# Summing modulation vectors over partitions: VectorE transpositions and four small matmuls in place of one-hot matmuls

## The chip, the cores and the metric

The kernel runs on one core of one Trainium2 chip. The time is device microseconds of one execution on that core; the time before is the median of three runs. A profile of one further execution is read below. TensorE is the matmul engine, VectorE and ScalarE the two elementwise engines, SyncE (SP) the queue that issues nearly all loads.

## The reference

Two layers of a diffusion transformer work on 256 latent tokens `x` and 256 context tokens `ctx`, both 1024 wide and in float32. Each layer is a SwiGLU feed-forward, a mixer (attention, pooling, Fourier) and a second feed-forward. Nine modulation vectors of 1024 values, each for the latent stream (from `c`) and for the context stream (from `c_ctx`), shift, scale and gate them:

```python
mx = jnp.split(jax.nn.silu(c) @ ada_w[layer] + ada_b[layer], N_MOD, axis=-1)
mc = jnp.split((jax.nn.silu(c_ctx) @ ada_w[layer] + ada_b[layer])[None, :], N_MOD, axis=-1)
x = x + 0.5 * mx[2][:, None] * swiglu(modulate(rms_norm(x), mx[0], mx[1]), ffn1_w_gu[layer], ffn1_w_down[layer])
...                                   # the same for ctx with mc, then the mixer and the second feed-forward
return rms_norm(x) * final_gain
```

`ada_w` is (2, 1024, 9216). The change concerns how `silu(c) @ ada_w` is summed, nothing else.

## The kernel before

Activations lie transposed in `xT`: 128 partitions by 8 chunks of 1024 features by 512 columns (256 latent, 256 context tokens). Every large matmul is done three times, on a high and a low half of each operand in float32r (`mm3`, L404 to L406). Weights come through a feeder: SP loads blocks `raw` of 1 MB, ScalarE rounds a half block to `a` (L193), VectorE subtracts to get the low half (L171).

A feed-forward (`ffn`) runs a gate/up loop over 22 blocks of 128 hidden features, two at a time. For each, VectorE multiplies the gate by the up product out of PSUM (L701), ScalarE rounds it, VectorE subtracts the low half (L706). After blocks 5, 9, 13 and 17 a batch of the down projection runs (`down`), whose results VectorE scales by a gate from `modT` and adds to `xT` (L738). Behind the loop come `down(16, 18)` and `down(18, 22)`.

The modulation vectors of a feed-forward's groups are computed beside the loop, on VectorE: `ada_stream` loads blocks of 128 x 1024 of `ada_w` into two buffers `ada` (SP, L584). A block k is the k-th 128 rows of one vector's matrix; it multiplies by a column of `c32` and adds into an accumulator of 128 x 1024, one for each stream that needs the vector (L603 for the first block, L605 for the other seven). A unit is 16 such products for two accumulators. What is left is a sum over the 128 partitions: `ada_post`, once for each unit, does four matmuls with one-hot columns `hot` (L629), which put the sums into one row of each quarter of a PSUM bank; after the group's last unit ScalarE copies the bank, four matmuls transpose it (L641) and VectorE adds the bias into `modT` (L647). There are 14 units with 28 accumulators in six groups: three groups of one, three and three units (14 accumulators) beside the first feed-forward of layer 0, one of three beside its second, and two of three and one beside the first of layer 1.

What sets the order is a planner in Python, `Sched`: `S.pe(ns)` advances its clock by what a piece of TensorE work is meant to take, and tasks written as generators are resumed when their `yield`ed delay is over on that clock. Each engine's queue is then as the program was recorded. `ada_stream` yields `ada_pace` between products (2200 ns in layer 0's first feed-forward), and `need_ada` runs whatever is still missing at once, all delays left out. Such calls stand before `down` (L722) and behind the gate/up loop, for all groups of this feed-forward:

```python
for group in ada_groups[l, w]:
    for unit in group:
        for l_, m_, _ in unit:
            need_ada(l_, m_)
preload(AF.Sqrt)
feed.limit = 8
down(16, 18, [streams], False)
```

Of the kernel before, what the change touches and what calls it, by code (L numbers as in the profile page):

```python
# [10 lines left out]
F32 = mybir.dt.float32  # L11
F32R = mybir.dt.float32r
AF = mybir.ActivationFunctionType
ALU = mybir.AluOpType
AX = mybir.AxisListType

P = 128
D = 1024
KD = D // P
# [210 lines left out]
def tile_hybrid_dit(  # L230
# [7 lines left out]
    nc = tc.nc  # L238
    cst = ctx.enter_context(tc.tile_pool(name="cst", bufs=1))
    wp = ctx.enter_context(tc.tile_pool(name="wp", bufs=1))  # L240
    sb = ctx.enter_context(tc.tile_pool(name="sb", bufs=1))
    psp = ctx.enter_context(tc.tile_pool(name="psp", bufs=8, space=bass.MemoryType.PSUM))
    ctx.enter_context(tc.manual_schedule())
    S = Sched()
    uid = [0]

    def nid(s):
        uid[0] += 1
        return f"{s}{uid[0]}"

    def psum():
        return psp.tile([P, 512], F32, name=nid("ps"), tag="ps")

    def t2(dt=F32, w=512):
        return sb.tile([P, w], dt, name=nid("t2_"), tag="t2", bufs=T2_BUFS)

    def t1(dt=F32, w=256):
        return sb.tile([P, w], dt, name=nid("t1_"), tag="t1", bufs=6)

    def a4(dt=F32, w=1024):  # L260
        return sb.tile([P, w], dt, name=nid("a4_"), tag="a4", bufs=TILE_BUFS)
# [7 lines left out]
    mm = nc.tensor.matmul  # L269
# [3 lines left out]
    ident = small[:, 0:128]  # L273
# [3 lines left out]
    chC = small[:, 512:640]  # L277
    chS = small[:, 640:768]
    sel = small[:, 768:770]
    hot = cst.tile([P, 3, 32], F32, name="hot", tag="hot")  # L280
    epsb = cst.tile([P, 1], F32, name="epsb", tag="epsb")
    dummy = cst.tile([P, 2], F32, name="dummy", tag="dummy")
    c32 = cst.tile([P, KD, 32], F32, name="c32", tag="c32")
    modT = [cst.tile([P, 72, 2], F32, name=f"modT{l}", tag=f"modT{l}") for l in range(2)]
    vecT = [cst.tile([P, 82], F32, name=f"vecT{l}", tag=f"vecT{l}") for l in range(2)]
# [249 lines left out]
    ada_run = {}  # L535

    def mod_fix(l, m, c0, c1, ss=(0, 1)):
        v = modT[l][:, c0:c1, ss[0]:ss[-1] + 1]
        if m in (1, 4, 7):
            nc.vector.tensor_scalar_add(v, v, 1.0)  # L540
        if m in (2, 8):
            nc.vector.tensor_scalar_mul(v, v, 0.5)
# [29 lines left out]
    def ada_stream(groups, pace):  # L572
        blocks = [
            (g, n, e, k) for g in range(len(groups)) for n in range(len(groups[g]))
            for e in range(len(groups[g][n])) for k in range(KD)
        ]
        loaded = {}

        def load(i):
            if i < len(blocks):  # L580
                g, n, e, k = blocks[i]
                l, m, _ = groups[g][n][e]
                raw = sb.tile([P, 1024], F32, name=nid("ada"), tag="ada", bufs=ADA_BUFS)
                nc.sync.dma_start(out=raw, in_=ada_w[l, k * P:(k + 1) * P, m * 1024:(m + 1) * 1024])  # L584
                loaded[i] = (raw, S.t)

        for i in range(ADA_BUFS):
            load(i)
        for i, (g, n, e, k) in enumerate(blocks):
            l, m, ss = groups[g][n][e]  # L590
            if k == 0:
                if e == 0:
                    accs = []
                    if n == 0:
                        sums, bank = [], []
                accs.extend((a4(), l, m, s) for s in ss)
            raw, at = loaded.pop(i)
            while S.t < at + ADA_LAG and not force[0]:
                yield pace
            for acc, _, _, s in accs[-len(ss):]:  # L600
                sc = c32[:, k, s:s + 1]
                if k == 0:
                    nc.vector.tensor_scalar_mul(acc, raw, sc)  # L603
                else:
                    nc.vector.scalar_tensor_tensor(  # L605
                        out=acc, in0=raw, scalar=sc, in1=acc, op0=ALU.mult, op1=ALU.add,
                    )
                yield pace if i >= 8 else min(pace, 1400)
            load(i + ADA_BUFS)
            if k == KD - 1 and e == len(groups[g][n]) - 1:  # L610
                more = n < len(groups[g]) - 1
                task = S.add(ada_post(groups[g], n, accs, bank, list(sums)), 4000)
                accs = None
                sums.append(task)
                if not more:
                    for unit in groups[g]:
                        for l_, m_, _ in unit:
                            ada_run[l_, m_] = task

    def ada_post(group, n, accs, bank, before):  # L620

        for task in before:
            S.finish(task)
        last = n == len(group) - 1
        if not bank:
            bank.append(psum())
        ps = bank[0]
        for j in range(4):
            mm(ps[32 * j:32 * j + 32, :], hot[:, n, :], accs[j % 2][0][:, (j // 2) * 512:(j // 2 + 1) * 512],  # L629
               start=(n == 0), stop=last)  # L630
        S.pe(925)
        bank.append([(None,) + slot[1:] for slot in accs])
        del accs
        if not last:
            return
        sbt = t2()
        nc.scalar.copy(sbt, ps)
        yield 2000
        tp = psum()
        for i in range(4):  # L640
            nc.tensor.transpose(tp[:, i * P:(i + 1) * P], sbt[:, i * P:(i + 1) * P], ident)  # L641
        S.pe(4 * 117)
        t4 = tp.rearrange("p (i u s r) -> p i u s r", i=4, u=2, s=2)
        for r, slots in enumerate(bank[1:]):
            for j, (_, l, m, s) in enumerate(slots):
                c0 = m * 8
                nc.vector.tensor_tensor(  # L647
                    out=modT[l][:, c0:c0 + 8, s].rearrange("p (u i) -> p i u", u=2),
                    in0=t4[:, :, :, j, r],
                    in1=vecT[l][:, c0:c0 + 8].rearrange("p (u i) -> p i u", u=2),  # L650
                    op=ALU.add,
                )
        for unit in group:
            for l, m, ss in unit:
                mod_fix(l, m, m * 8, m * 8 + 8, ss)
                ada_ok.add((l, m))
# [19 lines left out]
    def ffn(l, w, streams, h_tasks, tail, early=None):  # L676
# [7 lines left out]
        def start_ada():  # L684
            if ada_groups[l, w]:
                ada_run["task"] = S.add(ada_stream(ada_groups[l, w], ada_pace[l, w]), 500)
# [557 lines left out]
    nc.vector.memset(epsb, EPS)  # L1244
    nc.vector.memset(dummy, 0.5)
    nc.vector.memset(c32, 0.0)
    nc.vector.memset(hot, 0.0)
    for n in range(3):
        nc.vector.memset(hot[:, n, n:n + 1], 1.0)
    zero = t1()  # L1250
    nc.vector.memset(zero, 0.0)
    ada_first(0)
# [2 lines left out]
    ada_first(1)  # L1255
    pc = psum()
    nc.tensor.transpose(pc[:, :16], crow[:16, :], ident[:16, :16])
    nc.scalar.activation(
        out=c32[:, :, 0:2], in_=pc[:, 0:16].rearrange("p (s k) -> p k s", s=2), func=AF.Silu
    )  # L1260
# [91 lines left out]
    for l in range(2):  # L1352
        last = l == 1
# [257 lines left out]
```

## Time and profile before

| | |
|---|---|
| median of 3 runs | 1603.69 us (1601.97 to 1603.72) |
| profiled execution | 1601.59 us, its span 1599.5 us |
| TensorE busy | 1579.3 us, 99% of the span |
| VectorE busy | 1078.4 us, 67% |
| ScalarE busy | 601.5 us, 38% |
| chain of work that ended last | TensorE 96%, VectorE 2% |

Busy time of matmuls is modelled, and neighbours overlap: a 128x512 matmul is listed with some 390 ns, and the next starts 227 ns later. So for TensorE the starts, or the pieces of the chain, tell what an instruction displaces. A matmul on plain float32 operands stands in two records. An idle time in brackets names the instruction that ended it.

### The profile page before, as it was taken

To read this page: it belongs to the slowest core of one execution; us is meant where nothing else is said; L and a number is where in the kernel's file an instruction comes from. 1 tells how busy PE (TensorE), PEld (TensorE's weight loads), DVE (VectorE), ACT (ScalarE), POOL (GpSimd) and SP (SyncE) were. 2 spreads that over 40 slices of the span, in tenths; PEclk is the share of its full clock that TensorE was granted. 3 is DMA by queue.
4 is the path that set the end of the run, shared out by engine and by line. 5 is a ranking of instruction groups with operands and counts; after the bars stand their busy time and mean duration, and the time that the engine had idled before them with its cause. 6 is when DMAs were issued, how large, how long until landed. Compare 5 with 4: busy or idle time off the path is not lost.

```text
span 1599.5 us, 20723 instructions
## 1 busy us (share of the span) xinstructions
PE 1579.3 (99%) x8359; PEld 1321.1 (83%) x8359; DVE 1078.4 (67%) x1672; ACT 601.5 (38%) x1003; POOL 0.8 (0%) x6
## 2 busy tenths in 40 slices
PE   7999999999999999999999999999999999999998
PEld 5888888888886898888888898888888898788886
DVE  4787878786857566766734576766656488776665
ACT  4422132123548452222222343232132356755554
POOL 0000000000000000000000000000000000000000
PEclk9999999999999999999999999999999999999999
DMA  9755465553012424534333315455555233346560
GB/s 333 258 182 203 141 236 174 194 187 117 33 42 66 132 106 159 180 132 159 112 112 106 107 58 185 165 194 201 184 203 178 83 110 95 116 150 229 188 208 30
DMA packets 149343, 241.68 MB, mean 151 GB/s; under 512 B 6484, under 2 KB 115712, under 8 KB 148992
## 3 DMA queue, kind: packets, MB, share of 16 engines
q1 hardware_dynamic: 147008, 238.71, 44.8%
q10 hardware_dynamic: 2240, 1.65, 0.3%
q8 instruction: 66, 1.08, 0.3%
q14 instruction: 29, 0.24, 0.0%
HBM read 239.30 MB, written 1.05 MB: 150 GB/s over the span
## 4 chain that ended last, share of the span: by engine, by line
PE 96%; DVE 2%; SPq 1%; DMA 1%; ACT 0%; issue 0%; ACTq 0%
PE ps L404 24%; PE ps L405 24%; PE ps L406 24%; PE ps L1376 5%; PE ps L1380 3%; PE ps L944 2%; PE ps L946 2%; PE ps L945 2%; PE ps L1165 1%; PE ps L1142 1%; PE ps L1430 1%; PE ps L1432 1%; PE ps L1431 1%; PE ps L629 1%; DMA a<-in_ada_w_dram 1%; SPq L304 1%
## 5 line engine op out<-in xcount | busy, mean ns | idle before, releaser
L404 PE MATMUL ps<-ahi,a 128*128 128x512 f32 (+1 forms) x1312 | 479.6, 366 | 0.8 <-ACT a L193 0.6
L405 PE MATMUL ps<-alo,a 128*128 128x512 f32 (+1 forms) x1312 | 477.2, 364 | 1.4 <-DVE alo L510 1.3
L406 PE MATMUL ps<-ahi,a 128*128 128x512 f32 (+1 forms) x1312 | 476.8, 363 | 1.5 <-DVE a L171 1.5
L171 DVE TENSOR_TENSOR a<-raw,a 128x1024 fp32r<-128x1024 f32 x300 | 361.6, 1222 | 144.6 <-ACT a L193 144.6
L193 ACT CAST a<-raw 128x1024 fp32r<-128x1024 f32 x300 | 304.5, 1044 | 200.7 <-PE ps L405 77.0
L404 PEld LDWEIGHTS ps<-ahi,a 128*128 128x128 f32 x1312 | 247.5, 189 | 48.0 <-issue 8.3
L605 DVE SCALAR_TENSOR_TENSOR a<-ada,c,a 128x1024 f32<-128x1024 f32 x196 | 249.0, 1279 | 48.0 <-DMA ada<-in_ada_w_dram 48.0
L405 PEld LDWEIGHTS ps<-alo,a 128*128 128x128 f32 x1312 | 247.6, 189 | 40.8 <-DVE alo L510 2.6
L406 PEld LDWEIGHTS ps<-ahi,a 128*128 128x128 f32 x1312 | 247.5, 189 | 40.9 <-DVE a L171 1.9
L404 PE MATMUL ps<-a,a 128*128 128x512 f32 (+1 forms) x624 | 223.8, 359 | 0.0
L406 PE MATMUL ps<-a,a 128*128 128x512 f32 (+1 forms) x624 | 222.5, 356 | 0.0
L405 PE MATMUL ps<-a,a 128*128 128x512 f32 (+1 forms) x624 | 222.4, 356 | 0.0
L738 DVE SCALAR_TENSOR_TENSOR xT<-ps,modT,xT 128x256 f32<-128x256 f32 x288 | 126.5, 479 | 74.0 <-PE ps L406 73.9
L703 ACT CAST a<-t 128x512 fp32r<-128x512 f32 x66 | 41.0, 622 | 269.0 <-DVE t L701 269.0
L404 PEld LDWEIGHTS ps<-a,a 128*128 128x128 f32 x624 | 117.9, 189 | 21.7 <-issue 5.0
L406 PEld LDWEIGHTS ps<-a,a 128*128 128x128 f32 x624 | 117.9, 189 | 17.0
L405 PEld LDWEIGHTS ps<-a,a 128*128 128x128 f32 x624 | 117.9, 189 | 16.8
L696 ACT ACTIVATE t<-ps 128x512 f32<-128x512 f32 x66 | 39.3, 599 | 223.4 <-PE ps L406 219.9
L701 DVE TENSOR_TENSOR t<-ps,t 128x512 f32<-128x512 f32 x66 | 45.3, 690 | 70.8 <-PE ps L406 63.4
L1376 PE MATMUL ps<-ahi,a 128*128 128x512 f32 x352 | 90.5, 392 | 0.7 <-DVE ahi L510 0.7
L1376 PEld LDWEIGHTS ps<-ahi,a 128*128 128x128 f32 x352 | 63.6, 189 | 12.0 <-DVE ahi L510 0.9
L506 ACT ACTIVATE ahi<-t,modT 128x256 fp32r<-128x256 f32 x88 | 43.6, 508 | 55.3 <-DVE t L503 55.2
(175 smaller groups left out, 1376.1 us busy)
## 6 DMA issues: line engine op xcount, KB each, us to landing
raw<-in_ffn_w_gu_dram SPq DMA_DIRECT2D x88, 1024.0 KB, 5.2
ada<-in_ada_w_dram SPq DMA_DIRECT2D x128, 512.0 KB, 5.5
raw<-in_ffn_w_down_dram SPq DMA_DIRECT2D x44, 1024.0 KB, 4.9
raw<-in_w_in_dram SPq DMA_DIRECT2D x10, 1024.0 KB, 5.2
a<-in_ada_w_dram SPq DMA_DIRECT2D x16, 512.0 KB, 10.0
raw<-in_w_out_dram SPq DMA_DIRECT2D x16, 256.0 KB, 4.4
raw<-in_w_out_dram SPq DMA_DIRECT2D x8, 512.0 KB, 5.4
raw<-tab_pool SPq DMA_DIRECT2D x2, 1024.0 KB, 4.8
```

What stands on the lines that cost most here:

```text
L171: self.nc.vector.tensor_sub(vl, src, vh.bitcast(F32))
L193: self.nc.scalar.copy(vh, src)
L404: mm(ps, whi, mhi, start=start, stop=False)
L405: mm(ps, whi, mlo, start=False, stop=False)
L406: mm(ps, wlo, mhi, start=False, stop=stop)
L506: nc.scalar.activation(out=ahi[:, d, seg_cols(s)], in_=t, func=AF.Identity, bias=mod(l, m, d, s))
L605: nc.vector.scalar_tensor_tensor(out=acc, in0=raw, scalar=sc, in1=acc, op0=ALU.mult, op1=ALU.add,)
L701: nc.vector.tensor_mul(a[:, :n], u[:, :n], sg[:, :n])
L703: nc.scalar.copy(at[:, 0:n], a[:, :n])
L738: nc.vector.scalar_tensor_tensor(out=xs, in0=ps[:, q * 256:(q + 1) * 256], scalar=mod(l, m0 + 2, d, s), in1=xs, op0=ALU.mult, op1=ALU.add,)
L1376: mm(ps, wt[0][:, k, :], ahi[:, k, :], start=(k == 0), stop=(k == KD - 1))
L1380: mm(ps[:, 0:256], wt[1][:, k, :], ahi[:, k, 0:256], start=False, stop=False)
```

## The change

The one-hot matmuls, the copy on ScalarE and the four transposing matmuls go. As soon as a unit's eighth block is added, each accumulator is taken in two halves of 128 x 512: VectorE transposes its 32 x 32 blocks into a `t2` buffer, then sums each row of 32 into 16 columns of `red`. Between these four instructions the stream yields 700 ns each. Only after a group's last unit does `ada_post` run: four matmuls with `fold` (128 x 32, four identity blocks under each other) add the four partition quarters, and VectorE adds the bias.

```diff
-                task = S.add(ada_post(groups[g], n, accs, bank, list(sums)), 4000)
...
+            if k == KD - 1:
+                for acc, l_, m_, s in accs[-len(ss):]:
+                    for h in range(2):
+                        tb = t2()
+                        nc.vector.transpose(tb, acc[:, h * 512:(h + 1) * 512])
+                        yield 700
+                        nc.vector.tensor_reduce(
+                            out=red[:, len(slots), h * 16:(h + 1) * 16], in_=tb.rearrange("p (b i) -> p b i", i=32),
+                            axis=AX.X, op=ALU.add,
+                        )
+                        yield 700
+                    slots.append((l_, m_, s))
+                if e == len(groups[g][n]) - 1:
+                    accs = None
+                    if n == len(groups[g]) - 1:
+                        task = S.add(ada_post(groups[g], red, list(slots)), 4000)
...
-    def ada_post(group, n, accs, bank, before):
...
-        for j in range(4):
-            mm(ps[32 * j:32 * j + 32, :], hot[:, n, :], accs[j % 2][0][:, (j // 2) * 512:(j // 2 + 1) * 512],
-               start=(n == 0), stop=last)
-        S.pe(925)
...
-        nc.scalar.copy(sbt, ps)
-        yield 2000
...
-            nc.tensor.transpose(tp[:, i * P:(i + 1) * P], sbt[:, i * P:(i + 1) * P], ident)
-        S.pe(4 * 117)
...
+    def ada_post(group, red, slots):
+
+        ps = psum()
+        n = len(slots)
+        for b in range(4):
+            mm(ps[32 * b:32 * b + 32, 0:n * 8].rearrange("p (n i) -> p n i", n=n), fold, red[:, 0:n, b:32:4],
+               start=True, stop=True)
+        S.pe(400)
+        yield 600
```

Where the planner's clock advances otherwise, the order moves. On VectorE, at the end of layer 0's first gate/up loop, before (`ps_2840` is the loop's last product, `a_376` an accumulator of the last unit, `ps_2880` the transposed sums):

```order
L605 SCALAR_TENSOR_TENSOR a_375_2521<-ada_2760,c_73,a_375_2521 128x1024
L605 SCALAR_TENSOR_TENSOR a_376_2522<-ada_2760,c_73,a_376_2522 128x1024
L171 TENSOR_TENSOR a_419_2809<-raw_2633,a_418_2808 128x1024
L701 TENSOR_TENSOR t_420_2836<-ps_2804,t_412_2769 128x512
L706 TENSOR_TENSOR a_421_2838<-t_420_2836,a_421_2838 128x512
L171 TENSOR_TENSOR a_424_2845<-raw_2671,a_423_2844 128x1024
L701 TENSOR_TENSOR t_426_2876<-ps_2840,t_416_2802 128x512
L647 TENSOR_TENSOR modT_74<-ps_2880,vecT_76 128x4x2 x6
```

The last two products of the last unit stand ahead of two more L701; behind the loop's last L701 comes the bias addition at once.

On VectorE at the same place, now (`ps_2836` is the loop's last product; `a_385`, `a_386` are the accumulators of the unit before the last, `a_441`, `a_442` those of the last):

```order
L603 SCALAR_TENSOR_TENSOR a_386_2554<-ada_2789,c_73,a_386_2554 128x1024
L615 STREAM_TRANSPOSE t_435_2866<-a_385_2553 128x512
L693 TENSOR_TENSOR t_436_2871<-ps_2836,t_424_2795 128x512
L617 TENSOR_REDUCE red_2208<-t_435_2866 128x16
L615 STREAM_TRANSPOSE t_438_2876<-a_385_2553 128x512
L617 TENSOR_REDUCE red_2208<-t_438_2876 128x16
L615 STREAM_TRANSPOSE t_439_2879<-a_386_2554 128x512
L617 TENSOR_REDUCE red_2208<-t_439_2879 128x16
L615 STREAM_TRANSPOSE t_440_2882<-a_386_2554 128x512
L617 TENSOR_REDUCE red_2208<-t_440_2882 128x16
L601 TENSOR_SCALAR a_441_2885<-ada_2826,c_73 128x1024
L601 TENSOR_SCALAR a_442_2886<-ada_2826,c_73 128x1024
```

Behind these stand fourteen products (L603 now, L605 before) for blocks two to eight of the last unit, then four transpositions with their row sums, then the bias addition; L693 is what was L701.

On TensorE, now, at the end of the same loop:

```order
L406 MATMUL ps_2836<-ahi,a_405_2652 128x512
L636 MATMUL ps_2927<-red_2208,fold 32x48 x4
L404 MATMUL ps_2942<-a_362_2372,a_410_2690 128x512
L405 MATMUL ps_2942<-a_362_2372,a_410_2690 128x512
L406 MATMUL ps_2942<-a_362_2372,a_411_2691 128x512
```

The four matmuls that read `red` stand between the loop's last matmul and the first of `down(16, 18)`; before, the one-hot matmuls stood 9 matmuls ahead of the loop's end and the four transpositions here.

## Rows read from the trace of the kernel before

**Rows 1.** The page: span, engines (share, instructions), granted clock in 40 slices.

```profile
span 1599.5 us, 20723 instructions
...
PE 1579.3 (99%) x8359; PEld 1321.1 (83%) x8359; DVE 1078.4 (67%) x1672; ACT 601.5 (38%) x1003; POOL 0.8 (0%) x6
...
PEclk9999999999999999999999999999999999999999
```

**Rows 2.** Groups by line: count, busy us, mean ns, idle before.

```profile
L605 DVE SCALAR_TENSOR_TENSOR a<-ada,c,a 128x1024 f32<-128x1024 f32 x196 | 249.0, 1279 | 48.0 <-DMA ada<-in_ada_w_dram 48.0
...
L701 DVE TENSOR_TENSOR t<-ps,t 128x512 f32<-128x512 f32 x66 | 45.3, 690 | 70.8 <-PE ps L406 63.4 <-ACT t L696 7.3
...
L1118 DVE TENSOR_REDUCE st<-ps 128x1 f32<-128x512 f32 (+1 forms) x40 | 27.2, 687 | 8.9 <-PE ps L1115 8.7
...
L603 DVE TENSOR_SCALAR a<-ada,c 128x1024 f32<-128x1024 f32 x28 | 20.7, 748 | 4.9 <-DMA ada<-in_ada_w_dram 4.8
...
L629 PE MATMUL ps<-a,hot 128*32 128x512 f32 x112 | 14.9, 605 | 0.0
...
L641 PE MATMUL ps<-small,t 128*128 128x128 f32 x24 | 3.6, 271 | 0.0
```

**Rows 3.** Chain that ended last, in order: start us, us, engine and line.

```profile
31.77 0.80 PE ps L561 x8
...
370.41 1.00 PE ps L629 x8
371.41 0.43 PE ps L404
371.84 0.23 PE ps L405
...
373.68 0.44 PE ps L641 x4
```

**Rows 4.** VectorE in order of time, 362 to 375 us: start us, us, instruction.

```profile
362.07 2.48 DVE L605 SCALAR_TENSOR_TENSOR a<-ada,c,a 128x1024 f32<-128x1024 f32 x2 [3.10 <-DMA ada<-in_ada_w_dram]
...
373.72 0.69 DVE L701 TENSOR_TENSOR t<-ps,t 128x512 f32<-128x512 f32 x1 [3.06 <-PE ps L406]
374.33 0.53 DVE L647 TENSOR_TENSOR modT<-ps,vecT 128x8 f32<-128x8 f32 x6
```

**Rows 5.** TensorE in order of time, near 5, 22 and 104 us.

```profile
4.76 0.26 PE L1257 MATMUL ps<-small,t 16*128 16x16 f32 x1 [4.76 <-DMA small<-tab_small]
...
22.55 0.38 PE L406 MATMUL ps<-ahi,a 128*128 128x256 f32 x1 [0.76 <-DVE a L171]
22.77 0.28 PE L404 MATMUL ps<-ahi,a 128*128 128x256 f32 x1
...
104.54 0.39 PE L404 MATMUL ps<-a,a 128*128 128x512 f32 x1
```

**Rows 6.** Landings of the `ada` loads: all; 299 to 310; 330 to 370 us.

```profile
DMA to landing us min/median/max: 3.4/5.5/10.0
...
DMA to landing us min/median/max: 4.6/4.6/4.6
...
DMA to landing us min/median/max: 5.6/6.0/6.3
```

**Rows 7.** VectorE in order of time, 95 to 101 us.

```profile
95.95 1.22 DVE L171 TENSOR_TENSOR a<-raw,a 128x1024 fp32r<-128x1024 f32 x1
97.09 0.75 DVE L603 TENSOR_SCALAR a<-ada,c 128x1024 f32<-128x1024 f32 x1
97.75 0.69 DVE L701 TENSOR_TENSOR t<-ps,t 128x512 f32<-128x512 f32 x1
99.12 0.69 DVE L706 TENSOR_TENSOR a<-t,a 128x512 fp32r<-128x512 f32 x1 [0.68 <-ACT a L703]
100.07 1.23 DVE L171 TENSOR_TENSOR a<-raw,a 128x1024 fp32r<-128x1024 f32 x1 [0.26 <-ACT a L193]
```

**Rows 8.** Stretch: us, then PE, PEld, DVE, ACT, POOL busy us, clock, DMA, GB/s.

```profile
108.00:340.00 232.00, 232.00 (x1040) 187.48 (x1039) 183.81 (x220) 54.24 (x67) 0.00 (x0) 1.00 0.53 184
```

More of the change, by code (lines that the diff above doesn't have):

```diff
@@ L279, in tile_hybrid_dit @@
     sel = small[:, 768:770]
-    hot = cst.tile([P, 3, 32], F32, name="hot", tag="hot")
+    fold = cst.tile([P, 32], F32, name="fold", tag="fold")
     epsb = cst.tile([P, 1], F32, name="epsb", tag="epsb")
@@ L593, in ada_stream @@
                     accs = []
-                    if n == 0:
-                        sums, bank = [], []
                 accs.extend((a4(), l, m, s) for s in ss)
@@ L609, in ada_stream @@
             load(i + ADA_BUFS)
-            if k == KD - 1 and e == len(groups[g][n]) - 1:
-                more = n < len(groups[g]) - 1
-                task = S.add(ada_post(groups[g], n, accs, bank, list(sums)), 4000)
[L613 to L618, printed above, removed]
-    def ada_post(group, n, accs, bank, before):
[L622 to L627, printed above, removed]
-        for j in range(4):
-            mm(ps[32 * j:32 * j + 32, :], hot[:, n, :], accs[j % 2][0][:, (j // 2) * 512:(j // 2 + 1) * 512],
-               start=(n == 0), stop=last)
-        S.pe(925)
[L632 to L636, printed above, removed]
-        nc.scalar.copy(sbt, ps)
-        yield 2000
-        tp = psum()
-        for i in range(4):
-            nc.tensor.transpose(tp[:, i * P:(i + 1) * P], sbt[:, i * P:(i + 1) * P], ident)
-        S.pe(4 * 117)
[L643 to L652, printed above, removed]
@@ new lines, in ada_stream @@
+            if k == 0 and e == 0 and n == 0:
+                red = sb.tile([P, 6, 32], F32, name=nid("red"), tag="red", bufs=1)
+                slots = []
+            if k == KD - 1:
[14 more added lines that the diff above has]
+                        task = S.add(ada_post(groups[g], red, list(slots)), 4000)
+                        for unit in groups[g]:
+                            for l_, m_, _ in unit:
+                                ada_run[l_, m_] = task
@@ new lines, in ada_post @@
+    def ada_post(group, red, slots):
[6 more added lines that the diff above has]
+        yield 600
+        for j, (l, m, s) in enumerate(slots):
+            c0 = m * 8
+            nc.vector.tensor_tensor(
+                out=modT[l][:, c0:c0 + 8, s], in0=ps[:, j * 8:j * 8 + 8], in1=vecT[l][:, c0:c0 + 8], op=ALU.add,
+            )
@@ L1246, in tile_hybrid_dit @@
     nc.vector.memset(c32, 0.0)
-    nc.vector.memset(hot, 0.0)
-    for n in range(3):
-        nc.vector.memset(hot[:, n, n:n + 1], 1.0)
     zero = t1()
@@ L1257, in tile_hybrid_dit @@
     nc.tensor.transpose(pc[:, :16], crow[:16, :], ident[:16, :16])
+    nc.vector.tensor_reduce(
+        out=fold, in_=ident.rearrange("p (a j) -> p j a", a=4), axis=AX.X, op=ALU.add,
+    )
     nc.scalar.activation(
```

## The prediction

> **What bounds the kernel now.** I read the page first [rows 1]: TensorE is busy for 1579.3 of 1599.5 us, VectorE for 67%, and the granted clock is full in every slice. So a microsecond taken off TensorE's queue is a microsecond off the end, and one of VectorE costs nothing unless TensorE has to wait for its result. Then I read the groups by line [rows 2] for prices, the chain of waits around one modulation post for what it displaces [rows 3], and the end of the first feed-forward's gate/up loop on VectorE [rows 4], because there the order of the changed kernel differs most. The profiled execution took 1601.59 us, its span and 2.1 us around it; the median of the runs shown is 1603.69. I add the sum to the median.
>
> **Taken off TensorE.** A post is eight records of L629 and takes 1.00 us of the chain; the matmul behind it takes 0.43 where its neighbours take 0.23, so a post displaces 1.20 us [rows 3]. There are 112 records [rows 2], that is 14 posts: 14 x 1.20 = 16.8. The four transpositions of L641 displace 0.44 [rows 3]; there are 24 of them, in six groups: 2.6. Together 19.4 us leave a queue that is always full. The six copies on ScalarE (L637) go too; ScalarE is 38% busy, so they are worth nothing.
>
> **Put on TensorE.** Six times four small matmuls with `fold`, eight records each time. No row shows their shape. Eight records with two columns take 0.80 [rows 3]; four transpositions 0.44; a whole post 1.20. I take 0.7 (0.4 to 1.2), nearest to the first: 6 x 0.7 = 4.2 us.
>
> **Put on VectorE.** Each of 28 accumulators gets two 32x32 transpositions and two row sums of 128x512. For the row sum L1118 has the form: 687 ns [rows 2]. A transposition stands in no row; the bounds are half of L603 (0.37) and one L605 (1.28), and I take 0.69, the 128x512 add of L701, also one element read and one written per lane. A sum waits for its transposition just ahead, so a pair costs about 1.3; instructions that wait for nothing follow at 0.1 less than their length (L605 in twos: 2.48). The Trainium skill (VectorE: DVE Perf Modes, The three transpose paths) gives 311 ns for a 128x128 bf16 transposition; four of these would make 1.24 us, an estimate, and the sum would be 3.9 higher. No row here tests it.
>
> All 112 come to some 72 us of VectorE. Where nobody waits they are free. What matters is where they stand.
>
> **The place that decides: the end of the first gate/up loop.** The stream of layer 0 runs on the planner's clock. Each accumulator now yields four times 700 ns, 2.8 us, and this stream has 14: 39 us more. Before, its last block was done at 362.07 + 2.48 = 364.5 us and the loop's last product started at 373.72 [rows 4], a spare of 9.2. So it is now 30 us late, about one unit (eight blocks by two products by 2.2 us: 35). The order says the same: all eight blocks of the last unit stand behind the loop's last product, forced out by `need_ada` before `down(16, 18)`, and the four fold matmuls stand on TensorE between the loop's last matmul and that `down`. Before, nothing of the kind stood there: TensorE went on, and VectorE waited 3.06 us for it [rows 4].
>
> TensorE then waits for the whole run, as matmuls are not taken past a waiting one (the L406 that waited 0.76 for VectorE held the L404 behind it [rows 5]). The run can't start earlier, since VectorE's multiplication (L701) ahead of it waits for that last matmul. From the moment it ends: the multiplication 0.6; one sum and three pairs of the unit before, 0.6 + 3.9; two L603, 1.3. That is 6.4. Fourteen L605 at 1.2 are 16.8, the last four pairs 5.2: 28.4 us if no weights are waited for. But two buffers hold the blocks, and a load is issued only when VectorE has finished with the block two earlier. From issue to landing the rows have 3.4 at least, 5.5 in the middle, 4.6 for one that followed a larger load [rows 6]; in the run no other load is issued, so I take 4.0, with 0.2 for the two hand-overs. A pair of blocks then takes 2.4 + 4.2 = 6.6: the third block starts at 6.4 + 4.2 = 10.6, the fifth at 17.2, the seventh at 23.8, the eighth ends at 28.6, the pairs at 33.8. **TensorE waits 34 us** (no load waited for and the cheap transposition: 26; landings of 6.3, the longest near this place [rows 6]: 41; with the dear transposition 45).
>
> Behind the run on VectorE stand the correction of the last activation and the splits for `down(18, 22)`; `down(16, 18)` needs neither for its 48 matmuls, and its weights were split ahead. The next weight loads on SP are released by these splits and so move with TensorE: nothing more is lost.
>
> **The first fold.** It stands behind the matmul that ended the sixth gate/up block, before `down(0, 4)`. There VectorE has no slack: it went from L171 through L603 to the product at 97.75, waited 0.68 for ScalarE, and took the next split at 100.07 [rows 7]. With eight instructions more between 96.0 and TensorE's arrival (104.54 [rows 5] less the post and transposition gone, 102.9), the product moves to 99.6, the split with its wait for ScalarE to 102.0, and the last pair and a sum end near 105.1. TensorE waits 2.3 (0 to 3). The other four folds have their last sum ahead of a product that itself waits for TensorE, or the planner's 4 us of delay: 0.
>
> **The sum.** -16.8 - 2.6 + 4.2 + 2.3 + 34.0 = +21.1 us: 1603.7 + 21.1 = 1624.8, some **1625 us**, slower by 1.3%.
>
> **The rivals.** *The clock falls.* All rows have a full clock, even behind 4.8 us without work at the start [rows 1, 5]; none shows what TensorE does after 34 us of nothing. The 48 matmuls of `down(16, 18)` take 48 x 0.23 = 11 us. At the lower of the two levels (1.2 of 2.4 GHz) each takes twice that: if a third of them run so, +3.7, 1628.5; if all, 1636. The Trainium skill (TensorE: Matmul & The Clock Gate, The HAM clock gate) says that an engine left idle falls to half its clock and gets it back only when it has worked again; by that rule this rival is the outcome. For it: the wait is seven times longer than that one; against it: no row has a lower clock. *Matmuls pass the waiting folds.* Then the wait costs nothing, and with no first-fold wait the time is 1603.7 - 19.4 + 4.2 = 1588.5, faster. It decides as soon as `down(16, 18)` and what follows (11 us and more) can run ahead; the change breaks even at a wait of 19.4 - 4.2 - 2.3 = 12.9 us, which 31 instructions of the run could meet only at 0.42 us each, a third of L605. [rows 5] speaks against it. *Loads starve the run.* Landings of 6.3 us: a wait of 41, 1632. Against it: those landings stood behind larger loads.
>
> **How the numbers follow.** The forecast 0.50, the clock 0.37, starved loads 0.09, passing 0.04, in which I put 0.03 faster and 0.01 near no change. The range: the low end has the wait without loads and cheap transpositions, 26, folds at 0.4 and no wait at the first: 1603.7 - 19.4 + 2.4 + 26 = 1613, and the high end the clock down for all of `down(16, 18)`, 1636. I give 1614 to 1636. Slower by over 0.2% (what a measurement of this kernel can tell from no change, 3.2 us): 0.96; within: 0.01; faster: 0.03.
>
> **What will show it.** Right: one idle stretch of TensorE near 368 us, some 34 us long, its releaser the row sum; in it VectorE runs 16 products with waits for `ada` loads between them; L629 and L641 gone and no other idle stretch over 3 us. The price of a transposition stands in its own row. Wrong: if the stretch is under 13 us or missing, if transpositions are far from 0.69, or if TensorE loses time in small waits for L171 all over the stages where the stream runs (VectorE is busy for 183.81 of 232 us there [rows 8]), which I put at nothing.

## The result, and the profile after

The changed kernel takes **1623.77 us** (median of 4 runs, 1622.59 to 1626.44) beside 1603.70 us for the kernel before: ratio 1.0131, 95% interval 1.0119 to 1.0143. 1625 us were predicted. The profiled execution took 1626.44 us, its span 1624.6.

The page of the changed kernel (same columns as [rows 1]; the second PE line is the busy share in 40 slices):

```profile
span 1624.6 us, 20697 instructions
...
PE 1568.1 (97%) x8271; PEld 1322.3 (81%) x8271; DVE 1150.4 (71%) x1781; ACT 598.3 (37%) x997; POOL 0.8 (0%) x6
...
PE   7999999991999999999999999999999999999998
...
PEclk9999999995999999999999999999999999999999
```

TensorE is busy for 11.2 us less than in [rows 1] and the span is 25 us longer. Nearly all of the loss is in one slice of the forty: TensorE idle, and the granted clock at half. TensorE's waits of the changed kernel (engine, what waited <- what ended it: us in total, times, longest):

```profile
PE ps L636 <- DVE red L617: 37.0, 2, 35.0
PE ps L1246 <- DMA small<-tab_small: 4.8, 1, 4.8
```

Two waits of the new fold matmuls for row sums, and nothing else that is new. In order of time on TensorE (start us, us, instruction, idle before it):

```profile
369.12 0.39 PE L406 MATMUL ps<-ahi,a 128*128 128x512 f32 x1
404.55 0.39 PE L636 MATMUL ps<-red,fold 128*32 128x48 f32 x8 [35.05 <-DVE red L617]
404.87 0.80 PE L404 MATMUL ps<-a,a 128*128 128x512 f32 x1
405.46 0.63 PE L405 MATMUL ps<-a,a 128*128 128x512 f32 x1
...
410.58 0.51 PE L405 MATMUL ps<-a,a 128*128 128x512 f32 x1
410.93 0.40 PE L406 MATMUL ps<-a,a 128*128 128x512 f32 x1
411.17 0.40 PE L404 MATMUL ps<-a,a 128*128 128x512 f32 x1
```

Behind the wait, starts are 0.43 us apart where they are 0.23 elsewhere: 14 such gaps, in which 2.9 us are lost, then full speed. What VectorE did meanwhile (same columns; to be read beside [rows 4]):

```profile
369.25 1.28 DVE L603 SCALAR_TENSOR_TENSOR a<-ada,c,a 128x1024 f32<-128x1024 f32 x1
370.45 0.70 DVE L615 STREAM_TRANSPOSE t<-a 128x512 f32<-128x512 f32 x1
371.08 0.65 DVE L693 TENSOR_TENSOR t<-ps,t 128x512 f32<-128x512 f32 x1
371.65 0.67 DVE L617 TENSOR_REDUCE red<-t 128x16 f32<-128x512 f32 x1
372.24 0.70 DVE L615 STREAM_TRANSPOSE t<-a 128x512 f32<-128x512 f32 x1
372.97 0.69 DVE L617 TENSOR_REDUCE red<-t 128x16 f32<-128x512 f32 x1
...
376.25 1.41 DVE L601 TENSOR_SCALAR a<-ada,c 128x1024 f32<-128x1024 f32 x2
377.58 2.47 DVE L603 SCALAR_TENSOR_TENSOR a<-ada,c,a 128x1024 f32<-128x1024 f32 x2
381.57 2.48 DVE L603 SCALAR_TENSOR_TENSOR a<-ada,c,a 128x1024 f32<-128x1024 f32 x2 [1.52 <-DMA ada<-in_ada_w_dram]
384.30 2.48 DVE L603 SCALAR_TENSOR_TENSOR a<-ada,c,a 128x1024 f32<-128x1024 f32 x2 [0.25 <-DMA ada<-in_ada_w_dram]
387.93 2.48 DVE L603 SCALAR_TENSOR_TENSOR a<-ada,c,a 128x1024 f32<-128x1024 f32 x2 [1.16 <-DMA ada<-in_ada_w_dram]
...
403.81 0.69 DVE L617 TENSOR_REDUCE red<-t 128x16 f32<-128x512 f32 x1
405.01 0.53 DVE L642 TENSOR_TENSOR modT<-ps,vecT 128x8 f32<-128x8 f32 x6 [0.51 <-PE ps L636]
```

The eight blocks of the last unit run in one piece, two blocks every 6.36 us because each pair waits for its weights, then four transpositions with their sums. The prices of the new operations, groups by line as in [rows 2] (L603 is now the product, L693 what was L701):

```profile
L615 DVE STREAM_TRANSPOSE t<-a 128x512 f32<-128x512 f32 x56 | 39.3, 702 | 0.0
L617 DVE TENSOR_REDUCE red<-t 128x16 f32<-128x512 f32 x56 | 38.2, 682 | 1.2
```

L629 and L641 of [rows 2] are gone.

### The profile page after: what moved, and what is told of

Same layout as the page of the kernel before. It is cut to its first block, busy times and chain, and to the rows that moved or that the text cites. A ratio compares the mean times of both kernels' runs of the same rounds, so it can differ in the third digit from the quotient of the medians.

```text
span 1624.6 us, 20697 instructions
## 1 busy us (share of the span) xinstructions
PE 1568.1 (97%) x8271; PEld 1322.3 (81%) x8271; DVE 1150.4 (71%) x1781; ACT 598.3 (37%) x997; POOL 0.8 (0%) x6
## 4 chain that ended last, share of the span: by engine, by line
PE 89%; DVE 7%; DMA 3%; ACT 1%; issue 0%; SPq 0%; ACTq 0%; DVEq 0%
PE ps L404 22%; PE ps L405 22%; PE ps L406 22%; PE ps L1368 5%; PE ps L1372 3%; DVE a L603 2%; DMA ada<-in_ada_w_dram 2%; PE ps L936 2%; PE ps L938 2%; PE ps L937 2%; PE ps L1157 1%; DVE a L171 1%; PE ps L1134 1%; PE ps L1422 1%; PE ps L1424 1%; PE ps L1423 1%
## 5 line engine op out<-in xcount | busy, mean ns | idle before, releaser
L404 PE MATMUL ps<-ahi,a 128*128 128x512 f32 (+1 forms) x1312 | 479.2, 365 | 0.6 <-ACT a L193 0.6
L405 PE MATMUL ps<-alo,a 128*128 128x512 f32 (+1 forms) x1312 | 477.9, 364 | 1.3 <-DVE alo L510 1.3
L406 PE MATMUL ps<-ahi,a 128*128 128x512 f32 (+1 forms) x1312 | 477.5, 364 | 1.5 <-DVE a L171 1.5
L404 PEld LDWEIGHTS ps<-ahi,a 128*128 128x128 f32 x1312 | 248.1, 189 | 41.4 <-issue 1.6
L406 PEld LDWEIGHTS ps<-ahi,a 128*128 128x128 f32 x1312 | 248.3, 189 | 40.9 <-DVE a L171 1.9
L405 PEld LDWEIGHTS ps<-alo,a 128*128 128x128 f32 x1312 | 248.2, 189 | 41.0 <-DVE alo L510 2.5
L603 DVE SCALAR_TENSOR_TENSOR a<-ada,c,a 128x1024 f32<-128x1024 f32 x196 | 247.9, 1278 | 23.5 <-DMA ada<-in_ada_w_dram 23.4
L404 PE MATMUL ps<-a,a 128*128 128x512 f32 (+1 forms) x624 | 224.5, 360 | 0.0
L405 PE MATMUL ps<-a,a 128*128 128x512 f32 (+1 forms) x624 | 223.5, 358 | 0.0
L406 PE MATMUL ps<-a,a 128*128 128x512 f32 (+1 forms) x624 | 223.4, 358 | 0.0
L404 PEld LDWEIGHTS ps<-a,a 128*128 128x128 f32 x624 | 118.6, 190 | 17.3
L406 PEld LDWEIGHTS ps<-a,a 128*128 128x128 f32 x624 | 118.6, 190 | 17.2
L405 PEld LDWEIGHTS ps<-a,a 128*128 128x128 f32 x624 | 118.6, 190 | 17.1
L693 DVE TENSOR_TENSOR t<-ps,t 128x512 f32<-128x512 f32 x66 | 45.1, 687 | 54.1 <-PE ps L406 46.3
L698 DVE TENSOR_TENSOR a<-t,a 128x512 fp32r<-128x512 f32 x66 | 45.3, 691 | 32.2 <-ACT a L695 31.6
```

Source lines behind the costliest of these rows:

```text
L404: mm(ps, whi, mhi, start=start, stop=False)
L405: mm(ps, whi, mlo, start=False, stop=False)
L406: mm(ps, wlo, mhi, start=False, stop=stop)
L603: nc.vector.scalar_tensor_tensor(out=acc, in0=raw, scalar=sc, in1=acc, op0=ALU.mult, op1=ALU.add,)
L693: nc.vector.tensor_mul(a[:, :n], u[:, :n], sg[:, :n])
L698: nc.vector.tensor_sub(at[:, 512:512 + n], a[:, :n], at[:, 0:n].bitcast(F32))
```

## The experiments

The theory was: the change is worth some 16 us on TensorE, and the order (when the planner lets VectorE do what) costs 38, by one wait in one place and the slow matmuls behind it. The first rival: VectorE is not free at all, and 72 us of work on it cost time wherever they stand. Each run stands beside the kernel before on the same chip, which took 1602.15 us beside the first four of the table, 1602.98 beside the next four and 1602.82 beside the last three. `half` leaves out half of the row sums; all others compute the whole.

| run | us | ratio to before, 95% interval | TensorE's waits for row sums |
|---|---|---|---|
| no_yield | 1610.39 | 1.0054 [1.0039, 1.0068] | 3.1, 7.8, 7.7, 0.9 |
| delay_alone | 1628.27 | 1.0162 [1.0147, 1.0177] | (old sums) 20.5 |
| warm | 1622.49 | 1.0131 [1.0114, 1.0148] | 2.2, 2.0 behind filler |
| pace1900 | 1609.10 | 1.0044 [1.0029, 1.0059] | 20.1 |
| late | 1608.50 | 1.0036 [1.0023, 1.0048] | 2.7 |
| late1900 | 1599.70 | 0.9980 [0.9971, 0.9990] | 0.2 |
| half | 1597.26 | 0.9962 [0.9947, 0.9977] | 1.1, 4.8, 0.9 |
| ny_bufs3 | 1599.13 | 0.9975 [0.9963, 0.9987] | 8.3, 2.5 in three |
| later | 1602.55 | 0.9999 [0.9990, 1.0009] | none |
| later_bufs3 | **1585.83** | **0.9896 [0.9881, 0.9911]** | none |
| before_bufs3 | 1609.53 | 1.0046 [1.0031, 1.0061] | (old sums) 3.0 |

**The delay without the work.** The kernel before, with the four delays for each accumulator and no operation added to VectorE:

```diff
+            if k == KD - 1:
+                for _ in range(4 * len(ss)):
+                    yield 700
```

> The kernel before with nothing but the planner's delays of the change: behind each accumulator's eighth block the stream yields four times 700 ns; one-hot matmuls and transpositions stay, VectorE gets no instruction more. In the order all eight blocks of the last unit then stand behind the loop's last product. Theory: TensorE waits at that place for two TENSOR_SCALAR (1.3 us) and fourteen products with the waits for loads, 1.9 + 2.4 + three cycles of 6.4 + 2.4, about 24 us, then for the copy on ScalarE, 0.7, and loses 2.8 to the lower clock: 1603.7 + 27 = 1631 us (1627 to 1635). Rival A (the loss comes from the VectorE instructions): 1604 us, no wait over 3 us.

It took 1628.27 us, 26 us more than before. The wait stands where it stood in the changed kernel, in front of the old sums (TensorE in order of time; the line numbers are those of this kernel):

```profile
394.67 3.02 PE L632 MATMUL ps<-a,hot 128*32 128x512 f32 x8 [20.52 <-DVE a L605]
```

So the planner's delays alone, by moving one unit behind the loop, make the kernel slower than the changed one is; the work on VectorE isn't needed for it. The time is in the expected range; the wait is 20.5 us where some 24 had been worked out.

**The work without the delay.** The changed kernel with the delays at zero, both of them in the loop over halves:

```diff
-                        yield 700
+                        yield 0
```

> The changed kernel with the four delays of each accumulator on the planner's clock set from 700 to 0; all instructions are the same, and in the order the last unit now ends ahead of the loop's last two products, with every fold inside a stage. Theory (the loss is the place of the last unit): TensorE's 35.1 us wait, the lower clock behind it (14 matmuls at 0.43 instead of 0.23, 2.8 us) and the first fold's 2.0 us go, VectorE stays busy for some 1150 us; 1623.8 - 35.1 - 2.8 - 2.0 = 1584 us. Rival A (the added VectorE work is what TensorE pays for, wherever it stands): bursts of eight instructions would keep at least half of the loss, 1604 us or more. Rival B (fewer one-hot matmuls gain nothing, since TensorE's time is set elsewhere): 1603.7.

It took 1610.39 us: 13 better than the changed kernel, but 26 above the theory's figure. The 35 us wait is gone, and three others are there (a fourth, later, is 0.85 us):

```profile
101.54 0.26 PE L636 MATMUL ps<-red,fold 128*32 128x16 f32 x8 [3.13 <-DVE red L617]
...
244.70 0.39 PE L636 MATMUL ps<-red,fold 128*32 128x48 f32 x8 [7.81 <-DVE red L617]
...
385.32 0.39 PE L636 MATMUL ps<-red,fold 128*32 128x48 f32 x8 [7.73 <-DVE red L617]
```

The ledger closes: 16.4 saved on TensorE (19.4 less six folds at 0.5), 19.5 of waits, and 5.1 of slow matmuls behind three of them (9, 9 and 7 gaps near 0.43) make +8.2; measured +8.2. VectorE was late for a plan that now counted none of its new work. The theory had no term for that, and the time lies where rival A had put it.

**The clock alone.** The changed kernel, with 36 matmuls on constants ahead of the third fold, to keep TensorE at work while it would wait:

```diff
+        if group[0] == [(0, 6, (0, 1))] or group[0] == both_of(0, 6):
+            wps = psum()
+            for i in range(36):
+                mm(wps, ident, small[:, 0:512], start=True, stop=True)
```

> The changed kernel with 36 matmuls of two constants into an unused PSUM tile on TensorE, between the first gate/up loop's last matmul and the third fold; by L1285's rows they take 36 x 0.92 = 33 us of the 35.1 that TensorE waits there, and the order of the other engines is the same. Theory (the engine's clock fell while it had nothing to do, and that cost 2.8 us): the granted clock stays full, the 14 matmuls behind the fold start 0.23 apart instead of 0.43, and the wait for the row sum is under 3 us; 1623.8 - 2.8 = 1621.0. Rival (the slow matmuls have another cause, the weights or the PSUM tile just written): they stay at 0.43, and the time at 1623.8 or above.

It took 1622.49 us, the same ratio to before as the changed kernel has: no gain that can be measured. The stretches say why (us, PE busy, granted clock, DMA share, GB/s):

```profile
392.00:400.00 8.00, 7.66 (x18) 1.00 0.12 47
400.00:404.00 4.00, 2.34 (x14) 0.83 0.02 4
404.00:408.00 4.00, 4.00 (x14) 0.74 0.12 22
408.00:416.00 8.00, 8.00 (x42) 1.00 0.73 251
```

The filler ran at the full clock, but it ended 2.00 us before the fold could start, and even this left ten slow gaps, 1.7 us, in place of 14 with 2.9. The first fold of this run waited 2.18 us, with nine slow gaps behind it where the changed kernel had none. So what the filler saved here was lost there, and the run doesn't tell in microseconds what the clock alone costs; it does show that the matmuls behind the third fold are slow in fewer gaps when TensorE had work until just before.

**A shorter interval.** The changed kernel with products planned closer:

```diff
-    ada_pace = {(0, 0): 2200, (0, 1): 4400, (1, 0): 3200}
+    ada_pace = {(0, 0): 1900, (0, 1): 4400, (1, 0): 3200}
```

> The changed kernel with the stream's delay between products set from 2200 to 1900 ns in the first feed-forward alone: in the order 17 instead of 31 instructions of the stream stand behind the loop's last product (nine products, four transpositions, four row sums). Theory (TensorE waits for what stands behind that product, and no more): 0.6 + 1.2 + the products with their loads to about 14.5, + 5.4 = 20 us of waiting instead of 35, the lower clock as before: 1623.8 - 15 = 1609 us (1605 to 1613). Rival (the wait is set by the loads' rate or by an engine other than VectorE): it stays near 35 us, 1624.

1609.10 us, as expected: 17 of the stream's instructions stand behind the loop's last product instead of 31, the wait is 20.13 us instead of 35.05, and the first fold no longer waits. Up to here the order explains what happens, except in no_yield.

**The last unit's rest behind the loop.** The changed kernel, with the third group no longer forced before `down(16, 18)`, at either interval:

```diff
-        for group in ada_groups[l, w]:
+        for group in ada_groups[l, w][:2] if (l, w) == (0, 0) else ada_groups[l, w]:
```

> The changed kernel, but the loop behind layer 0's first gate/up loop that issues what is left of the modulation stream now issues only the first two units' rest; the third unit's products stay in the stream and are given out beside the down projections and the mixer that follow, and its fold stands among the mixer's matmuls. Nothing of the computation is left out. Theory (the 35.05 us wait of TensorE and the slow clock after it come from the place at which the rest is issued in one piece, and VectorE has room behind the loop): both go, the first fold's 1.9 us stay: 1623.8 - 35.0 - 2.8 = 1586 us; up to 10 us more if the spread products delay what the norm and the mixer wait for on VectorE: 1588 (1585 to 1597), ratio to the kernel before 0.99, no wait of TensorE on a row sum above 3 us. Rival (VectorE has no room there either): a wait of 15 us or more shows up at the fold, or at the norm's or the mixer's tiles, and the time stays at 1604 us or above.

> As the kernel with the third unit's rest given out behind the loop, and with the first stage's stream interval at 1900 ns in place of 2200, so that more of the stream lies inside the loop. Nothing of the computation is left out. Theory (order and room both): the first fold's wait of 1.9 us goes as it did with 1900 ns alone, the last unit's fold finds its row sums done: 1585 us (1582 to 1595), at or 1 to 3 us below the kernel with 2200 ns. Rival (at 1900 ns VectorE is over-full in the loop, and what it has in hand behind the loop, 17 rows of the stream, meets the norm's work): waits of 5 to 20 us for VectorE behind the loop, 1592 to 1606 us.

Both missed the theory's 1588 and 1585. In `late` the 35 us wait for the row sums is gone (2.7 us are left at the first fold), and TensorE waits in the norm behind the loop instead (waits from 386 to 440 us, the stretch of TensorE there, and what VectorE did ahead of the squares, `ssq`, that the norm waits for):

```profile
PE ps L486 <- DVE ssq L454: 6.4, 2, 5.3
PE ps L496 <- DVE st L492: 1.4, 1, 1.4
```

```profile
400.00:440.00 40.00, 36.60 (x174) 0.77 0.27 86
```

```profile
398.03 1.28 DVE L603 SCALAR_TENSOR_TENSOR a<-ada,c,a 128x1024 f32<-128x1024 f32 x1 [1.30 <-DMA ada<-in_ada_w_dram]
...
400.35 0.41 DVE L454 TENSOR_TENSOR ssq<-ssq,t 128x256 f32<-128x256 f32 x1
```

VectorE has products of 1.27 us, one of them behind a wait for its weights, between the short steps of the norm, and it is busy for 61.24 of the 66 us from 374 on. TensorE's clock falls with it: 0.77 over 40 us, which is worth 9.2 us at most. In `late1900` the same norm waits 9.5 us for the squares. Both times lie in the rival's ranges. In `late` the waits in the norm, 7.8 us, are half of the 15 that the rival named; the slow clock and a wait of 1.7 us of the third fold for ScalarE can make up for the rest, but no run parts them. `late1900` is the first version below the kernel before (0.998).

**Less work, or earlier weights.** What fills VectorE? In no_yield it was busy for 276.5 of the 319 us from 55 to 374, and waited for weights for another 32.4. `half` takes work away, `ny_bufs3` takes the waits away; each is no_yield with the edit shown:

```diff
-                        nc.vector.transpose(tb, acc[:, h * 512:(h + 1) * 512])
+                        nc.vector.transpose(tb[:, 0:256], acc[:, h * 512:h * 512 + 256])
...
-                            out=red[:, len(slots), h * 16:(h + 1) * 16], in_=tb.rearrange("p (b i) -> p b i", i=32),
+                            out=red[:, len(slots), h * 16:(h + 1) * 16], in_=tb[:, 0:256].rearrange("p (b i) -> p b i", i=16),
```

> The changed kernel with the four planned costs of 700 ns set to 0, as in the run no_yield (1610.4 us), and each transposition and each row sum on 256 of its 512 columns: half of the rows' sums are left out, with about half of the time of these two kinds of operation (24 pairs until the third fold, some 0.65 us less each: 16 us). Same order of instructions on every engine. Theory (VectorE is full in the first gate/up loop: the folds of no_yield wait 19.5 us because VectorE runs behind its plan by its own work): the folds' waits fall from 19.5 us to under 6 us: 1594 us (1589 to 1599). Rival (the folds wait for a reason that VectorE's own work does not change, such as a fixed delay of the pair or the landing of the weights): the waits stay at 15 to 20 us: 1606 to 1611 us.

```diff
-ADA_BUFS = 2
+ADA_BUFS = 3
...
-T2_BUFS = 8
+T2_BUFS = 6
```

> The changed kernel with the four planned costs of 700 ns set to 0, as in the run no_yield (1610.4 us), with three buffers instead of two for the modulation weights, and six instead of eight of one other pool to make room. Nothing is left out. In no_yield VectorE waits 35.5 us in 19 waits for these weights in the stage from 55 to 385 us. Theory (it is room on VectorE as a whole, waits for weights included, that is missing): the waits for weights fall by 20 us or more and the folds' waits by as much, to under 6 us: 1594 us (1589 to 1600). Rival A (VectorE's own work alone sets the lag; the waits for weights are time in which it had nothing older to do): folds still wait 15 to 20 us, 1606 to 1611 us. Rival B (the loads are late for the speed at which they are moved, a third buffer does not start them earlier where it counts): waits for weights stay above 30 us, 1606 to 1611 us.

Both come out 11 to 13 us below no_yield, inside the theory's ranges, 3 and 5 above its figures: in `half` the folds still waited 6.9 us, in `ny_bufs3` 10.8, where under 6 had been expected. `half` has the order of no_yield; `ny_bufs3` has not. A block that is loaded earlier is also given out earlier by the planner, and the first three folds stand 36, 48 and 48 matmuls further forward on TensorE than in no_yield, some 8, 11 and 11 us (counted in the traces, L404 to L406 ahead of each fold). So 8.3 us of wait at the first fold stand beside a question put 8 us sooner, and the next two, put 11 us sooner, waited 0.33 us each instead of 7.8 and 7.7. VectorE's stretch from 55 to 374 us and its waits for weights there, `no_yield` first:

```profile
55.00:374.00 319.00, 276.51 (x340) 0.98 0.54 184
```

```profile
DVE a L603 <- DMA ada<-in_ada_w_dram: 32.4, 18, 3.2
```

and `ny_bufs3`:

```profile
55.00:374.00 319.00, 287.23 (x362) 0.98 0.55 188
```

```profile
DVE a L603 <- DMA ada<-in_ada_w_dram: 0.5, 2, 0.2
```

With a third buffer VectorE gets 22 instructions further in the same stretch. So in no_yield it was full: 309 of 319 us were its work or its waits for weights, and taking away either shortens TensorE's waits.

**The folds further back.** `later` is no_yield with each fold planned 14 us behind its last sum instead of 4, and the third group not forced; `later_bufs3` is the same with the third buffer:

```diff
-                        task = S.add(ada_post(groups[g], red, list(slots)), 4000)
+                        task = S.add(ada_post(groups[g], red, list(slots)), 14000)
```

> The changed kernel with the four planned costs of 700 ns set to 0, as in the run no_yield (1610.4 us, folds waiting 3.13, 7.81, 7.73 and 0.85 us), each group's task with its fold due 14 us behind the last row sum instead of 4 us, and the third group not forced behind the loop. VectorE's instructions and the loads stay as in no_yield; the first three folds stand 21, 42 and 39 matmuls (4.8, 9.5 and 8.9 us) further back on TensorE. Nothing is left out. Theory (VectorE is late for its plan by a bounded 8 us or so; the waits are only a matter of where TensorE has the folds): the waits go, and with them the slow clock behind them (some 2 us each for three): 1610.4 - 19.5 - 5 = 1586 us (1584 to 1591). Rival (VectorE falls further behind the longer TensorE runs undisturbed, since it has no room at all): the folds still wait 3 us or more each: 1595 to 1610 us.

> The same with three buffers instead of two for the modulation weights, and six instead of eight of the other pool, as in the run ny_bufs3 (1599.1 us, whose first fold waits 8.32 us and whose other folds wait 2.5 us together). The first three folds stand 46, 42 and 39 matmuls further back. Nothing is left out. Theory: the 10.8 us of waits and some 3 us of slow clock go: 1585 us (1583 to 1589). Rival (the first fold waits for a VectorE that is held up by weights at the start of the stage, whatever the place): 3 us or more left at the first fold: 1589 to 1597 us.

In `later` no fold waits, and yet it takes 1602.55 us: 8 better than no_yield, not 24. TensorE waits for something else that VectorE makes, the low halves of the weights:

```profile
273.07 0.79 PE L406 MATMUL ps<-ahi,a 128*128 128x512 f32 x1 [3.29 <-DVE a L171]
...
346.20 0.79 PE L406 MATMUL ps<-ahi,a 128*128 128x512 f32 x1 [5.58 <-DVE a L171]
```

With two buffers and no pauses VectorE falls behind until its next product that TensorE needs is late, here the weight halves. The rival's time and its mechanism hold, but not its place: it had named the folds. With the third buffer VectorE is busy for 294 us of the same stretch and waits 0.8 for weights, and TensorE waits for it no longer than in the kernel before, under 2 us at any line (`later_bufs3`, its new folds at 230 us and the page):

```profile
230.01 0.39 PE L406 MATMUL ps<-ahi,a 128*128 128x512 f32 x1
230.33 0.36 PE L636 MATMUL ps<-red,fold 128*32 128x48 f32 x8
230.62 0.50 PE L404 MATMUL ps<-ahi,a 128*128 128x512 f32 x1
230.96 0.39 PE L405 MATMUL ps<-alo,a 128*128 128x512 f32 x1
```

```profile
span 1582.4 us, 20699 instructions
```

**1585.83 us, 0.9896 of the kernel before** (1585 expected), the best of all. This is what the edit is worth when its order fits: 17.0 us, beside 16.4 by the rows of TensorE. Beside no_yield the first three folds stand almost where they stood (9 matmuls further back, 6 and 9 further forward): the longer delay takes back what the third buffer's plan had moved forward, and it is the buffer that has the sums ready there in time.

**The buffers alone.** The kernel before, with the third buffer:

> The kernel before, unchanged but for three buffers instead of two for the modulation weights, and six instead of eight of the other pool. Nothing is left out. It tells how much of a gain with three buffers belongs to the change and how much to the buffers alone. Theory (the kernel before has no wait of TensorE on VectorE that a third buffer could take away; VectorE's 38.1 us of waits for weights cost it nothing): 1604 us (1602 to 1606), or up to 8 us more where its first sums, which now stand 37 matmuls further forward, are waited for. Rival (the third buffer itself is worth 10 us): 1594 us or below.

1609.53 us, 0.5% slower: the sums stand 37 matmuls further forward there, and TensorE waits for the first (3.01 us, with 2.4 of slow matmuls behind it; some 1.3 of the 6.7 us stay open). The gain of `later_bufs3` is therefore not the buffer's; it needs the change with the buffer and the later fold, as neither of the last two is enough without the other (`ny_bufs3`, `later`). Two runs are missing: the changed kernel, its delays kept, with the third buffer and the later fold, and the kernel before with the buffer and its sums moved back. The latter has little to gain, as TensorE is busy for 99% of the span before.

## Why the prediction was right, step by step

- **What leaves TensorE, 19.4 us; six folds, 4.2 expected.** In [rows 3]'s manner, a fold displaces 0.50: from L406 at 230.01 to L405 at 230.96 there are 0.95 us with the fold between, 0.45 without. Six make 3.0. The net, 16.4, agrees with `later_bufs3`, where no fold waits: 17.0.
- **A transposition, 0.69 taken:** 0.702, near the price of the other 128x512 instructions here (L617, 0.682). The prediction's estimate of 1.24 us, scaled up from the Trainium skill's figure for a 128x128 bf16 transposition (VectorE: DVE Perf Modes, The three transpose paths), doesn't hold for this shape in float32; the figure itself no run here tests.
- **The wait at the end of the loop, 34.0:** 35.05. The third block started 12.1 us after TensorE stopped (369.5 to 381.57), taken 10.6: the last multiplication began only at 371.08, since a product and a transposition stood ahead of it. The cycle of two blocks was 6.36, taken 6.6 (the landings in the chain of waits are 3.79, 3.76 and 3.57 us, taken 4.0). The two misses go opposite ways.
- **The first fold, 2.3:** 1.94. The other four waited for nothing, as said.
- **The clock, given as a rival at 0.37:** it came true beside the forecast, in its smaller form. A third of the 48 matmuls were to run at half speed, +3.7; 14 did, +2.9. Against it the prediction had "All rows have a full clock, even behind 4.8 us without work at the start", and this was a misreading: the page's clock row reads full there, but the spacing doesn't. In the trace of the kernel before, the transpositions behind that idle start begin 0.21 us apart, the same ones 10 us later 0.11 apart (in the lines below, 16 in 3.68 us and 8 in 1.09). So there was an example of a slow TensorE behind an idle stretch, and it spoke for this rival. The Trainium skill's rule (TensorE: Matmul & The Clock Gate, The HAM clock gate) gave the outcome, and the trace agrees: clock 0.52 of full from 405 to 411 us, then 1.00. TensorE of the kernel before, in order of time:

```profile
6.19 3.68 PE L441 MATMUL ps<-small,a 128*128 128x128 f32 x16 [1.17 <-DMA a<-in_x_dram]
...
15.69 1.09 PE L441 MATMUL ps<-small,a 128*128 128x128 f32 x8
```

- **The sum.** By the rows: -19.4 + 3.0 + 1.9 + 35.1 + 2.9 = +23.5; the medians are 20.1 apart, the two profiled executions 24.9, of which 2.2 is a lower clock in the first 55 us of this one execution (0.94; before 1.00): the matmul behind the first fold starts 3.0 us later than in [rows 5], and what left and came there makes only 0.8. That leaves 22.7, near the rows. The forecast of +21.1 was closer to the medians than its parts deserve, and this is luck: it left out the clock, 2.9, and 1.1 of the long wait, it took folds and first wait 1.6 too dear, and the medians lie 3.4 closer together than the rows say, which is within the 3.9 us from the fastest to the slowest run.
- **The step that was wrong without consequence: "where nobody waits they are free".** The prediction read VectorE's 184 of 232 us [rows 8] as room, and gave the wait in small pieces no price. In the changed kernel this holds: with the planner's pauses, and the last unit behind the loop, VectorE has 267.4 us of work and 15.5 of waits for weights in the 319 us from 55 to 374. Without the pauses it fails: with its waits for weights (38.8 us in the kernel before from 55 to 374 us, 38.1 of them ahead of L605, beside 253.6 of work) VectorE was taken for 292 of 319 us of the stage already, and 28 pairs at 1.34, 37.5 us, do not fit unless those waits shrink. That the 35 us wait is this overflow, gathered in one place by the delays, is not shown: `delay_alone` has a wait of 20.5 us there without any added work, so most of it is the delays' own. VectorE's stretch and its wait for weights in the kernel before:

```profile
55.00:374.00 319.00, 253.59 (x299) 1.00 0.55 189
```

```profile
DVE a L605 <- DMA ada<-in_ada_w_dram: 38.1, 22, 3.2
```

- **The size of the delay.** The prediction counted 2.8 us of planned time for each accumulator. The clock of the planner moves in steps of one `mm3` (three times 216 ns), so a delay of 700 is over only at the second step, 1.3 us; four are 5.2. It did no harm, since the place of the last unit was read from the order itself.

## What to carry to other kernels

Count an engine's waits for its own loads as taken time before calling the rest room: here VectorE's 67% of the span was 79% in the stage that mattered, and 92% with its waits for weights. From a 1.3% loss to a 1.0% gain it took three steps: the delays out (13 us), the folds later and the third group no longer forced (8 us), and one more load buffer (17 us, with 27 us of VectorE's waits for weights gone from the stage). A result that the bottleneck engine needs should be asked for as late as its consumer allows. If a wait moves to another line when one is taken away (row sums, then the norm's squares, then weight halves), the engine that is waited for may be full; then moving the place alone gains little, as in `later`.

## What the runs showed of the hardware

- After 35 us without work TensorE ran 14 matmuls 0.43 us apart, some 6 us (granted clock 0.52 of full), before it was at 0.23 again. Waits of 3.1, 7.8 and 7.7 us left 9, 9 and 7 such gaps (no_yield). Much shorter ones cost about as much: 2.74 us (`late`, first fold) and 2.18 us (`warm`, first fold) left nine, 2.00 us behind 31 us of filler (`warm`) ten. One of 1.94 us (the changed kernel's first fold) left none, its spacing stayed at 0.23.
- In each of the thirteen traces the first transpositions of the run (L441), behind some 6 us almost without work, start 0.21 us apart, and later ones 0.11, though the page's clock row reads 9 in that slice: the spacing tells more than the row does.
- Four float32 fold matmuls (eight records, 32 columns of the array, 48 values each) displace 0.50 us, less than half of a one-hot post with 512 values (1.20).
- A 32x32-block transposition of 128x512 float32 took 702 ns, a row sum over 32 of as many 682 ns; a pair where each needs the one ahead, 1.34 us.
